# The low halves of the split weights made by ACT and an accumulating DMA, instead of a subtraction on DVE

## The chip, the core and the metric

The kernel runs on one core of a Trainium2 chip, as one program on one input (one sequence of 1024 frames, 1024 channels, one layer). The metric is the device time of one execution in microseconds (us). Of the kernel before there are three timed executions: 2161.12, 2165.23 and 2161.25 us, median 2161.25 us. One further execution was taken with the hardware profiler.

Five engines work side by side, each going through its own list of instructions in order: PE multiplies matrices, DVE does elementwise work, ACT does elementwise functions and copies, POOL does some elementwise work and here mostly starts DMA transfers, SP only starts transfers. An instruction that has to wait holds up everything behind it in its engine's list. A DMA that an engine starts runs on its own afterwards, on 16 DMA engines that all queues share.

## What is computed

The reference is one layer of a sequence model: a modulated RMS norm, one wide projection, a short convolution branch and a state-space (SSD) branch with a gated norm, two output projections merged by sigmoid gates, one more projection, and then a squared-ReLU MLP. Cut to what matters for the time:

```python
u = rms_norm(x, ln1) * (1.0 + scale1) + shift1          # scale, shift, gate: c_act @ w_ada + b_ada
proj = u @ w_in                                         # 1024 x 11296
gl, cb, cc, cx, z, xbc, dt = jnp.split(proj, split_at, axis=-1)
p_conv = (cb * causal_depthwise_conv(cc * cx, conv_w)) @ w_conv_out
y = ssd_scan(...) ; y = gated_norm(y * silu(z))
p_ssm = y @ w_ssm_out                                   # 2048 x 1024
g_conv, g_ssm = jnp.split(sigmoid(gl), 2, axis=-1)
x = x + gate1 * ((g_conv * p_conv + g_ssm * p_ssm) @ w_o)
u2 = rms_norm(x, ln2) * (1.0 + scale2) + shift2
x = x + gate2 * (square(relu(u2 @ w_up)) @ w_down)      # 1024 x 4096 and 4096 x 1024
return rms_norm(x, final_norm)
```

All of it is in float32. Nearly all of the time goes into the matrix products with weights.

## The kernel before, in words

**Layout.** Channels lie on the 128 partitions, frames along the free dimension: a tile of 128 channels by 1024 frames, mostly handled as two halves of 512. Weights come from memory in tiles of 128 x 1024 floats (512 KB): eight blocks of 128 x 128.

**Split operands.** PE multiplies in the float32r format, which rounds its inputs. To keep the accuracy, each operand is split in two: the high part is the operand rounded to float32r, the low part is the operand minus its high part, rounded in turn. A product is then the sum of three matmuls: high by high, high by low, low by high. Activations are split where they are made; the weights must be split in the kernel, tile by tile.

**How a weight is split.** `load_w` (lines 90 to 97) takes the next weight: SP starts the load of `wraw` (three buffers), ACT casts it to `whi` (line 94), and DVE computes `wlo` = `wraw` - `whi` (line 96, recorded under the helper's line 43). `whi` and `wlo` have four buffers each, so a new weight can be split as soon as PE has done its last matmul with an older one whose buffer it takes. In `proj` (matmuls at lines 111, 112 and 114), the weight's low part is needed after four matmuls with its high part: two for each of the two halves of the frames. One weight tile feeds 48 matmuls there.

**Strassen pairs.** The gate (`gl`), the `z`, four of the eight convolution tiles and most of the up projection run in pairs of weight tiles through `strassen_pair` (line 136), with Strassen's scheme of seven products instead of eight, 12 matmuls each (line 145), 84 a pair. There are 33 pairs: 5 for the gates, 8 for z, 6 for the convolution, 14 for the up projection. Each pair splits four weights in `wsplit` (lines 148 to 153): `wa` (a weight as loaded), `w12` and `w34` (two tiles of sums that DVE forms from the loaded ones in `s12` and `s34`), and `wb` (half a tile). The seven products follow in this order: P1 with `wa`, P2 and P3 with `w12`, P4 with `w34`, P5 with `wa`, P6 with `w34`, P7 with `wb`. The results are combined by DVE (`cu`, `cq`, `cy`) and written out by ACT.

**The conditioning product.** `gemvs` (line 412) multiplies 32 tiles of `w_ada` with a vector. POOL starts the load into `wv` (one buffer), DVE multiplies and sums (line 291, called here the gemv). They are issued three to a pair from the third gate pair on to the last z pair. The next load waits until DVE has done the gemv before it.

**Order of the work.** The source is written stage by stage, but the order within each engine's list is set when the program is built, by a scheduler that simulates the engines with its own idea of durations and puts an instruction where it became ready there. A change of one operation so moves others.

The stages in time: statistics and the first norm with the first four gate tiles (to about 80 us); gate tiles 4 and 5 (to 106); gate, z and convolution pairs (to about 485); per head group the projections and the SSD scan, with the other convolution tiles between (to about 1100); the two output projections and `w_o` (to about 1440); four up tiles and the 14 up pairs (to about 1800); the down projection and the last norm.

Of the kernel before, what the change touches and what calls it, by code (L numbers as in the profile page):

```python
# [7 lines left out]
F32 = mybir.dt.float32  # L8
# [3 lines left out]
ALU = mybir.AluOpType  # L12
# [4 lines left out]
T = 1024  # L17
H = 512
# [19 lines left out]
def hybrid_trunk(tc, xT, par, hrows, crow, wada1, wada2, win, wdt, wco, wso, wo, wup, wdn, out):  # L38
    nc = tc.nc
    pe, act, dve, pool, sp = nc.tensor, nc.scalar, nc.vector, nc.gpsimd, nc.sync  # L40

    def tt(o, a, b, op, eng=dve):
        return eng.tensor_tensor(out=o, in0=a, in1=b, op=op)  # L43

    def stt(o, a, s, b, op0, op1):
        return dve.scalar_tensor_tensor(out=o, in0=a, scalar=s, in1=b, op0=op0, op1=op1)  # L46
# [38 lines left out]
    def load_raw(src):  # L85
        raw = wp.tile([P, T], F32, name="wraw", bufs=3)
        sp.dma_start(raw, src)
        return raw

    def load_w(src, raw=None, eng=dve):  # L90
        if raw is None:
            raw = load_raw(src)
        hi = wp.tile([P, T], F32R, name="whi")
        act.copy(hi, raw)  # L94
        lo = wp.tile([P, T], F32R, name="wlo")
        tt(lo, raw, hi.bitcast(F32), ALU.subtract, eng=eng)
        return hi, lo

    def split(hi, lo, src):
# [3 lines left out]
    def shift_split(hi, lo, src, col):  # L103
        act.activation(hi, src, AF.Identity, bias=col)  # L104
        return stt(lo, src, col, hi.bitcast(F32), ALU.add, ALU.subtract)
# [3 lines left out]
    def mm3(outs, wh, wl, xh, xl, start, stop):  # L109
        for o, h_, l_ in zip(outs, xh, xl):  # L110
            pe.matmul(o, lhsT=wh, rhs=h_, start=start, stop=False)  # L111
            pe.matmul(o, lhsT=wh, rhs=l_, start=False, stop=False)  # L112
        for o, h_ in zip(outs, xh):
            last_mm[0] = pe.matmul(o, lhsT=wl, rhs=h_, start=False, stop=stop)  # L114
# [21 lines left out]
    def strassen_pair(tp_, w0, w1, X, evac):  # L136
        a, b, c, d = [mm.tile([P, H], F32, name="mm") for _ in range(4)]
        r0, r1 = load_raw(w0), load_raw(w1)
        k1, k2 = hs

        def prod(o, w, i, x, first, last):
            for k in range(4):
                s_ = slice(i * H + k * P, i * H + k * P + P)
                for j, (l_, r_) in enumerate(((w[0], x[k][0]), (w[0], x[k][1]), (w[1], x[k][0]))):
                    last_mm[0] = pe.matmul(o, lhsT=l_[:, s_], rhs=r_, start=first and k == j == 0,  # L145
                                           stop=k == 3 and j == 2, skip_group_check=True)

        def wsplit(src, n=T):
            hi = wp.tile([P, T], F32R, name="whi")[:, :n]
            act.copy(hi, src)  # L150
            lo = wp.tile([P, T], F32R, name="wlo")[:, :n]
            tt(lo, src, hi.bitcast(F32), ALU.subtract)
            return hi, lo

        wa = wsplit(r0)
        s12 = tp_.tile([P, T], F32, name="s12", bufs=1)
        s34 = tp_.tile([P, T], F32, name="s34", bufs=1)
        tt(s12[:, k1], r1[:, k1], r1[:, k2], ALU.add)
        tt(s12[:, k2], s12[:, k1], r0[:, k1], ALU.subtract)
        w12 = wsplit(s12)  # L160
        tt(s34[:, k1], r0[:, k1], r1[:, k1], ALU.subtract)
        tt(s34[:, k2], r0[:, k2], s12[:, k2], ALU.subtract)
        w34 = wsplit(s34)
        wb = wsplit(r1[:, k2], H)

        cu, cq, cy = [tp_.tile([P, H], F32, name=n) for n in ("cu", "cq", "cy")]
        prod(a, wa, 0, X["11"], True, False)
        act.copy(cu, a)  # L168
        prod(b, w12, 1, X["T2"], True, True)
        tt(cu, b, cu, ALU.add)  # L170
        prod(c, w12, 0, X["T1"], True, False)
        tt(cq, c, cu, ALU.add)
        prod(d, w34, 0, X["T3"], True, False)
        tt(cq, d, cq, ALU.add)
        evac(1, 1, cq)
        prod(a, wa, 1, X["21"], False, True)
        evac(0, 0, a)
        prod(c, w34, 1, X["22"], False, True)
        tt(cy, c, cu, ALU.add)
        evac(0, 1, cy)  # L180
        prod(d, wb, 0, X["T4"], False, True)
        tt(cu, d, cu, ALU.add)
        evac(1, 0, cu)
# [86 lines left out]
    wa = {}  # L270

    def load_ada(j):
        for q in (1, 0):
            wa[j, q] = p0.tile([P, T], F32, name="wada", bufs=8)
            sp.dma_start(wa[j, q], wada1[j, :, q])
# [6 lines left out]
    raws = [load_raw(win[f]) for f in (0, 1)]  # L282
# [7 lines left out]
    def gemv(w_, o):  # L290
        return dve.tensor_tensor_reduce(out=w_, in0=w_, in1=cb, scale=0.5, scalar=prm[:, BADA + o:BADA + o + 1],  # L291
                                        op0=ALU.mult, op1=ALU.add, accum_out=mcol[:, o:o + 1])
# [32 lines left out]
    ws = []  # L325
# [5 lines left out]
    for j in range(KT):  # L331
        if j > 1:
            load_ada(j)
        if j in (0, 1):
            with tc.issue_after(rdy.ins), (tc.issue_after(rbc.ins) if j else contextlib.nullcontext()):
                for f in range(2):
                    ws.append(load_w(win[2 * j + f], raws[2 * j + f]))
        with tc.issue_after(rdy.ins) if j else contextlib.nullcontext():
            gemv(wa[j, 1], 8 + j)
            gemv(wa[j, 0], j)  # L340
        stt(s1c[:, j:j + 1], mcol[:, 8 + j:9 + j], 1.0, prm[:, LN1 + j:LN1 + j + 1], ALU.add, ALU.mult)
        for h in (0, 1):
            x_ = xt[j][h]
            stt(x_, x_, s1c[:, j:j + 1], rbs[h], ALU.mult, ALU.mult)
            rdy = shift_split(uh[j][h], ul[j][h], x_, mcol[:, j:j + 1])
        if j == 0:
            continue
        for jj in ((0, 1) if j == 1 else (j,)):
            for h in (0, 1):
                for f in range(4):  # L350
                    mm3([sps[f][h]], ws[f][0][:, jj * P:jj * P + P], ws[f][1][:, jj * P:jj * P + P],
                        [uh[jj][h]], [ul[jj][h]], jj == 0, jj == KT - 1)
# [10 lines left out]
    p0.release()  # L363
    p0x.release()
    ws = [load_w(win[f]) for f in (4, 5)]
    tks, X = [], {n: [] for n in ("11", "21", "22", "T1", "T2", "T3", "T4")}
    dc1 = dcs[:, 8:12]
# [78 lines left out]
    for f in range(6, 16, 2):  # L446
        ts_ = [glp.tile([P, T], F32, name="glt") for _ in (0, 1)]

        def gl_ev(i, h, src):
            act.activation(ts_[i][:, hs[h]], src, AF.Tanh, scale=0.5)  # L450

        if f == 8:
            dt_chain()
        elif f > 8:
            gemvs(3)
        strassen_pair(pe1, win[f], win[f + 1], X, gl_ev)
        for i in (0, 1):
            act.dma_start(gl_d[f + i], ts_[i])
    for g in range(NG):
        ts_ = [glp.tile([P, T], F32, name="glt") for _ in (0, 1)]  # L460

        def z_ev(i, h, src):
            t = ts_[i][:, hs[h]]
            act.activation(t, src, AF.Tanh, scale=0.5)
            stt(t, t, 1.0, src, ALU.add, ALU.mult)

        gemvs(3)
        strassen_pair(pe1, win[gtile(g) + 4], win[gtile(g) + 5], X, z_ev)
        for i in (0, 1):
            act.dma_start(z_d[2 * g + i], ts_[i])  # L470
# [9 lines left out]
    for f0 in range(0, NYE, 2):  # L480
        ys_ = []
        for f in (f0, f0 + 1):
            y = glp.tile([P, T], F32, name="glt")
            v = pe1.tile([P, T + 32], F32, name="wv", bufs=1)
            pool.memset(v[:, 0:2], 0.0)
            keep = {}

            def v_ev(i, h, src):
                if (i, h) == (1, 1):
                    keep[0] = src  # L490
                elif (i, h) == (0, 0):
                    act.copy(y[:, hs[0]], src)
                else:
                    tt(v[:, 2 + H * h:2 + H * h + H], src, keep[0] if h else y[:, hs[0]], ALU.mult)

            strassen_pair(pe1, win[17 + 3 * f], win[16 + 3 * f], X, v_ev)
            taps(y, v, f)
            ys_.append(y)

        def y_ev(i, h, src):  # L500
            tt(ys_[i][:, hs[h]], src, ys_[i][:, hs[h]], ALU.mult)

        strassen_pair(pe1, win[18 + 3 * f0], win[21 + 3 * f0], X, y_ev)
        for i in (0, 1):
            act.dma_start(yc_d[f0 + i], ys_[i])
# [312 lines left out]
    ws = [load_w(wup[i]) for i in range(4)]  # L818
# [48 lines left out]
    for b in range(8):  # L867
# [21 lines left out]
        else:  # L889
            ws = [load_w(wdn[b, i]) for i in range(4)]  # L890
# [90 lines left out]
```

## Time and profile before

| | us |
|---|---|
| three timed executions | 2161.12, 2161.25, 2165.23 |
| the profiled execution's own time | 2164.64 |
| its span, first to last instruction | 2162.9 |
| PE busy | 2121.5 (98% of the span) |
| DVE busy | 1398.5 (65%) |
| ACT busy | 869.2 (40%) |
| POOL busy | 108.9 (5%) |

The span leaves 1.7 us of the profiled execution's time outside it. Busy times of PE overlap: a matmul of 128 x 512 is shown with about 390 ns, and the next one starts some 227 ns after it (between 345.83 and 346.51 us three matmuls start). So for PE a count of matmuls in a window tells more than its busy time: at full pace it does 222 or 223 in 50 us. The DMA share is the mean busy share of the 16 DMA engines.

### The profile page before, as it was taken

What the parts mean: (1) busy time and instruction counts of PE and PEld (TensorE: products, weight loads), DVE (VectorE), ACT (ScalarE), POOL (GpSimd) and SP (SyncE); (2) the same over time, 40 slices, a digit from 0 to 9 for tenths busy, and PEclk for the clock granted to TensorE, in tenths of its full rate; (3) what the DMA queues carried; (4) which work ended last, traced back from release to release, by engine and by line L of the source; (5) the groups of instructions that cost most, each with busy time, mean ns of one, the idle gap of its engine ahead of it and who ended that gap; (6) DMA issues with size and microseconds to landing.
All of it is one profiled execution on the core that took longest, in us unless ns stands there. A gap on an engine that the chain in (4) does not pass through costs nothing.

```text
span 2162.9 us, 26045 instructions
## 1 busy us (share of the span) xinstructions
PE 2121.5 (98%) x9920; PEld 1731.0 (80%) x9920; DVE 1398.5 (65%) x2144; ACT 869.2 (40%) x1436; POOL 108.9 (5%) x200
## 2 busy tenths in 40 slices
PE   7999999999999999999999999999999999999998
PEld 4778778888888888887878888888788888888887
DVE  7876787764786856767884658656655545444444
ACT  4433233334564636445663421334444453211212
POOL 0000000000000000000000000011000000000003
PEclk8999999999999999999999999999999999999999
DMA  8235654123233323233356676532333336422212
GB/s 303 74 106 194 201 180 165 60 87 110 63 98 108 83 93 103 71 109 91 98 184 230 224 265 212 196 126 90 131 111 117 108 117 224 124 90 88 88 39 78
DMA packets 115471, 283.27 MB, mean 131 GB/s; under 512 B 10465, under 2 KB 45665, under 8 KB 115346
## 3 DMA queue, kind: packets, MB, share of 16 engines
q1 hardware_dynamic: 86882, 187.02, 27.1%
q0 software_dynamic: 16192, 58.73, 8.0%
q10 hardware_dynamic: 12272, 35.85, 4.2%
q8 instruction: 78, 1.28, 0.2%
q14 instruction: 47, 0.39, 0.1%
HBM read 218.45 MB, written 63.11 MB: 130 GB/s over the span
## 4 chain that ended last, share of the span: by engine, by line
PE 81%; issue 11%; DVE 3%; DMA 2%; ACT 1%; POOL 1%; SPq 0%; POOLq 0%; DVEq 0%; ACTq 0%
PE mm L145 21%; PE mm L112 18%; PE mm L111 18%; PE mm L114 18%; PE B L600 2%; PE B L605 1%; PE C L622 1%; DMA wv<-in_wada 1%; DVE wada L291 1%; PE A L577 1%; DMA x<-in_xT 1%; POOL wv L415 1%; DVE ul L46 1%; DVE x L46 0%; DMA hr<-hid_d 0%
## 5 line engine op out<-in xcount | busy, mean ns | idle before, releaser
L111 PE MATMUL mm<-uh,whi 128*128 128x512 f32 x768 | 303.3, 398 | 3.7 <-ACT uh L104 3.2
L112 PE MATMUL mm<-ul,whi 128*128 128x512 f32 x768 | 304.7, 397 | 0.0
L94 ACT CAST whi<-wraw 128x1024 fp32r<-128x1024 f32 x125 | 131.4, 1051 | 428.4 <-PE mm L112 404.2
L145 PE MATMUL mm<-t,whi 128*128 128x512 f32 x944 | 292.2, 391 | 7.2 <-ACT whi L150 4.4
L114 PE MATMUL mm<-uh,wlo 128*128 128x512 f32 x768 | 246.2, 396 | 1.9 <-DVE wlo L43 1.9
L43 DVE TENSOR_TENSOR wlo<-wraw,whi 128x1024 fp32r<-128x1024 f32 (+1 forms) x191 | 215.6, 1129 | 40.6 <-ACT whi L94 34.3
L145 PEld LDWEIGHTS mm<-t,whi 128*128 128x128 f32 x944 | 177.4, 189 | 46.9 <-DVE cq L43 5.1
L46 DVE SCALAR_TENSOR_TENSOR y<-mm,mcol,y 128x512 f32<-128x512 f32 (+1 forms) x136 | 92.4, 715 | 158.0 <-PE mm L114 157.9
L145 PE MATMUL mm<-t,wlo 128*128 128x512 f32 x472 | 183.5, 390 | 0.0
L111 PEld LDWEIGHTS mm<-uh,whi 128*128 128x128 f32 x768 | 144.4, 189 | 35.7 <-ACT uh L104 5.3
L114 PEld LDWEIGHTS mm<-uh,wlo 128*128 128x128 f32 x768 | 144.8, 189 | 32.3 <-DVE wlo L43 2.3
L112 PEld LDWEIGHTS mm<-ul,whi 128*128 128x128 f32 x768 | 145.0, 189 | 29.4 <-issue 0.9
L112 PE MATMUL mm<-hid,whi 128*128 128x512 f32 (+1 forms) x416 | 154.9, 374 | 0.0
L111 PE MATMUL mm<-hid,whi 128*128 128x512 f32 (+1 forms) x416 | 153.9, 373 | 0.0
L111 PE MATMUL mm<-ys,whi 128*128 128x512 f32 x384 | 148.8, 397 | 2.3 <-DVE gt L46 1.8
L112 PE MATMUL mm<-ys,whi 128*128 128x512 f32 x384 | 149.0, 396 | 0.0
L46 DVE SCALAR_TENSOR_TENSOR cacc<-raw,hw,cacc 128x1024 f32<-128x1024 f32 x96 | 122.8, 1279 | 27.8 <-ACT cacc L552 27.4
L145 PE MATMUL mm<-s,whi 128*128 128x512 f32 x448 | 137.9, 389 | 0.7 <-ACT cu L168 0.7
L114 PE MATMUL mm<-hid,wlo 128*128 128x512 f32 (+1 forms) x416 | 130.0, 373 | 0.0
L114 PE MATMUL mm<-ys,wlo 128*128 128x512 f32 x384 | 122.6, 394 | 0.0
L594 ACT ACTIVATE seg<-acb,acum 128x128 f32<-128x128 f32 x256 | 81.9, 392 | 98.7 <-PE B L600 91.2
L43 DVE TENSOR_TENSOR wlo<-s,whi 128x1024 fp32r<-128x1024 f32 x66 | 80.5, 1220 | 52.4 <-ACT whi L150 52.4
(272 smaller groups left out, 3963.1 us busy)
## 6 DMA issues: line engine op xcount, KB each, us to landing
wraw<-in_win SPq DMA_DIRECT2D x87, 512.0 KB, 3.6
wv<-in_wada POOLq DMA_DIRECT2D x32, 512.0 KB, 3.8
acb<-ac_d SPq DMA_DIRECT2D x64, 256.0 KB, 4.6
wraw<-in_wup SPq DMA_DIRECT2D x32, 512.0 KB, 3.5
hr<-hid_d POOLq DMA_DIRECT2D x32, 512.0 KB, 4.6
wraw<-in_wdn SPq DMA_DIRECT2D x32, 512.0 KB, 3.5
hid_d<-hid POOLq DMA_DIRECT2D x28, 512.0 KB, 4.3
gt<-gl_d SPq DMA_DIRECT2D x24, 512.0 KB, 4.3
```

Source lines behind the costliest of these rows:

```text
L43: return eng.tensor_tensor(out=o, in0=a, in1=b, op=op)
L46: return dve.scalar_tensor_tensor(out=o, in0=a, scalar=s, in1=b, op0=op0, op1=op1)
L94: act.copy(hi, raw)
L111: pe.matmul(o, lhsT=wh, rhs=h_, start=start, stop=False)
L112: pe.matmul(o, lhsT=wh, rhs=l_, start=False, stop=False)
L114: last_mm[0] = pe.matmul(o, lhsT=wl, rhs=h_, start=False, stop=stop)
L145: last_mm[0] = pe.matmul(o, lhsT=l_[:, s_], rhs=r_, start=first and k == j == 0, stop=k == 3 and j == 2, skip_group_check=True)
L291: return dve.tensor_tensor_reduce(out=w_, in0=w_, in1=cb, scale=0.5, scalar=prm[:, BADA + o:BADA + o + 1], op0=ALU.mult, op1=ALU.add, accu ...
L415: pool.dma_start(w_, wada2[i])
L577: pe.matmul(A[:, 0:P], lhsT=bf[:, cs], rhs=cf[:, cs], start=True, stop=True)
L594: act.activation(seg[:, r, :], acb[:, r, :], AF.Relu, bias=acum[:, c, hd:hd + 1], scale=-1.0)
L600: pe.matmul(Bk[o:o + 64, P * (r // 2):P * (r // 2) + P], lhsT=xd[:, r, :], rhs=seg[:, r, :], start=True, stop=True, skip_group_check=True)
```

## The change

A new helper `low` takes the place of DVE's subtraction. ACT writes the negated value, rounded to float32r, into `wlo` (a multiply by -1, line 91 of the changed kernel); then POOL starts a DMA that reads the unsplit value once more and adds it to what is in `wlo` (line 92). The source of that DMA is the weight in memory for a weight as loaded, and the tile `s12` or `s34` in the core's own memory for the two sums of a pair. The four weights of the first stage keep the subtraction on DVE.

```diff
-    def load_w(src, raw=None, eng=dve):
+    def low(lo, val, src):
+        act.mul(lo, val, -1.0)
+        pool.dma_start(lo, src, accum_op=ALU.add)
+
+    def load_w(src, raw=None, eng=None):
         if raw is None:
             raw = load_raw(src)
         hi = wp.tile([P, T], F32R, name="whi")
         act.copy(hi, raw)
         lo = wp.tile([P, T], F32R, name="wlo")
-        tt(lo, raw, hi.bitcast(F32), ALU.subtract, eng=eng)
+        if eng is None:
+            low(lo, raw, src)
+        else:
+            tt(lo, raw, hi.bitcast(F32), ALU.subtract, eng=eng)
         return hi, lo
...
-        def wsplit(src, n=T):
+        def wsplit(val, src, n=T):
             hi = wp.tile([P, T], F32R, name="whi")[:, :n]
-            act.copy(hi, src)
+            act.copy(hi, val)
             lo = wp.tile([P, T], F32R, name="wlo")[:, :n]
-            tt(lo, src, hi.bitcast(F32), ALU.subtract)
+            low(lo, val, src)
             return hi, lo
 
-        wa = wsplit(r0)
+        wa = wsplit(r0, w0)
...
-        w12 = wsplit(s12)
+        w12 = wsplit(s12, s12)
...
-        w34 = wsplit(s34)
-        wb = wsplit(r1[:, k2], H)
+        w34 = wsplit(s34, s34)
+        wb = wsplit(r1[:, k2], w1[:, k2], H)
...
-                    ws.append(load_w(win[2 * j + f], raws[2 * j + f]))
+                    ws.append(load_w(win[2 * j + f], raws[2 * j + f], dve))
```

In the built program 254 splits change: 254 subtractions leave DVE (221 of a whole tile, 33 of half a tile), ACT gets 254 more instructions, POOL starts 254 more DMAs. 66 of them read from `s12` and `s34`, 188 from the weights in memory (33 of these half a tile).

Three places of the built order. The first is ACT's list over one z pair, before; the names `whi` and `wlo` carry the number of the tile, `glt` and `cq`, `cy`, `cu` are the results of the pair ahead, `mm` its sums on PE.

```order
L150 CAST whi_1955<-wraw_1951 128x1024
L464 ACTIVATE glt_1793<-cq_1834 128x512
L150 CAST whi_1963<-s12_1959 128x1024
L464 ACTIVATE glt_1792<-mm_1803 128x512
L150 CAST whi_1969<-s34_1960 128x1024
L464 ACTIVATE glt_1792<-cy_1835 128x512
L150 CAST whi_1973<-wraw_1953 128x512
```

And the same stretch in the changed program:

```order
L157 CAST whi_1985<-wraw_1981 128x1024
L91 ACTIVATE wlo_1987<-wraw_1981 128x1024
L471 ACTIVATE glt_1819<-cq_1864 128x512
L157 CAST whi_1994<-s12_1990 128x1024
L471 ACTIVATE glt_1818<-mm_1829 128x512
L91 ACTIVATE wlo_1996<-s12_1990 128x1024
L157 CAST whi_2001<-s34_1991 128x1024
L91 ACTIVATE wlo_2003<-s34_1991 128x1024
L471 ACTIVATE glt_1818<-cy_1865 128x512
L157 CAST whi_2006<-wraw_1983 128x512
L91 ACTIVATE wlo_2008<-wraw_1983 128x512
```

Each cast is followed by the negated rounding of the same value; for `w12` (the tile from `s12`) one write-out of the pair ahead stands between the two.

The second is POOL's list from the end of its setup on, before: all loads of `wv`, then small memsets.

```order
masks.py:66 AFFINE_SELECT tri<-tri 128x128
L415 DMA wv<-in_wada 128x1024 x32
L485 MEMSET wv 128x2 x4
L671 MEMSET vv 128x2 x2
L547 MEMSET raw 128x3 x11
```

And two z pairs of it in the changed program:

```order
L422 DMA wv_1968<-in_wada2 128x1024
L92 DMA wlo_1987<-in_win 128x1024
L422 DMA wv_1971<-in_wada2 128x1024
L92 DMA wlo_1996<-s12_1990 128x1024
L92 DMA wlo_2003<-s34_1991 128x1024
L422 DMA wv_1974<-in_wada2 128x1024
L92 DMA wlo_2008<-in_win 128x512
L422 DMA wv_2116<-in_wada2 128x1024
L92 DMA wlo_2135<-in_win 128x1024
L422 DMA wv_2119<-in_wada2 128x1024
L92 DMA wlo_2144<-s12_2138 128x1024
L92 DMA wlo_2151<-s34_2139 128x1024
```

The four accumulating DMAs of a pair and three loads of `wv` now share POOL's list, so a load that waits for its gemv stands ahead of a weight's low part, and the other way round.

The third is PE's list where the products with `w12` begin (P2 into the first sum, P3 into the second), before:

```order
L145 MATMUL mm_1947<-uh30_114,wlo_1957 128x512
L145 MATMUL mm_1948<-t10_678,whi_1963 128x512
L145 MATMUL mm_1948<-t11_679,whi_1963 128x512
L145 MATMUL mm_1948<-t10_678,wlo_1965 128x512
L145 MATMUL mm_1948<-t10_702,whi_1963 128x512
L145 MATMUL mm_1948<-t11_703,whi_1963 128x512
```

And in the changed program:

```order
L152 MATMUL mm_1977<-uh30_114,wlo_1987 128x512
L152 MATMUL mm_1978<-t10_680,whi_1994 128x512
L152 MATMUL mm_1978<-t11_681,whi_1994 128x512
L152 MATMUL mm_1979<-t00_676,whi_1994 128x512
L152 MATMUL mm_1979<-t01_677,whi_1994 128x512
L152 MATMUL mm_1978<-t10_680,wlo_1996 128x512
```

Two matmuls of P3 with the high part were drawn ahead of the first one with the low part of `w12`, which is now the fifth matmul with that weight instead of the third.

## The prediction

> **What bounds the kernel now.** The first view is the page's busy times, the second the list of what PE waited for (total us, times, longest).
>
> ```profile
> PE 2121.5 (98%) x9920; PEld 1731.0 (80%) x9920; DVE 1398.5 (65%) x2144; ACT 869.2 (40%) x1436; POOL 108.9 (5%) x200
> PE st L310 <- DVE sacc L43: 8.1, 2, 5.6
> PE mm L145 <- ACT whi L150: 4.4, 1, 4.4
> ...
> PE mm L145 <- DVE cq L43: 3.0, 5, 1.3
> ...
> PE mm L114 <- DVE wlo L43: 1.9, 1, 1.9
> PE mm L111 <- DVE gt L46: 1.8, 1, 1.8
> ...
> PE C L657 <- DVE sql L43: 1.4, 1, 1.4
> PE B L600 <- DVE seg L43: 1.0, 1, 1.0
> ```
>
> PE is the bound, 98% of the span. Its 15 waits add up to about 35 us, and those on DVE outside the opening statistics (`cq`, `wlo`, `gt`, `sql`, `seg`) to 9.1 us. That is all a lighter DVE can give back. So the question is not what DVE saves, but whether the new way delivers `wlo` in time, and what it loads the DMA engines with. The third view, busy time by windows, has PE's matmul count behind its busy time and the DMA share as the last but one column.
>
> ```profile
> 200.00:250.00 50.00, 48.36 (x212) 39.35 (x211) 35.33 (x53) 13.91 (x19) 4.24 (x8) 1.00 0.57 191
> 400.00:450.00 50.00, 50.00 (x223) 41.38 (x222) 34.46 (x46) 13.59 (x16) 0.10 (x1) 1.00 0.24 74
> 1370.00:1390.00 20.00, 20.00 (x90) 16.55 (x89) 15.81 (x24) 7.05 (x10) 0.00 (x0) 1.00 0.52 163
> 1650.00:1700.00 50.00, 50.00 (x222) 41.40 (x221) 27.20 (x35) 25.57 (x36) 2.66 (x5) 1.00 0.28 95
> 1700.00:1750.00 50.00, 50.00 (x222) 41.41 (x221) 25.64 (x34) 22.01 (x32) 2.66 (x5) 1.00 0.35 119
> ```
>
> 50 us hold 222 matmuls, so one takes 0.225 us, a product of 12 takes 2.7 and a Strassen pair of 84 takes 18.9 us. The first row is pairs with three gemvs: the DMA engines are already busy 0.57 x 18.9 = 10.8 us of each pair. The second is convolution pairs (4.5 us), the last two up pairs (0.315 x 18.9 = 6.0 us).
>
> **The change part by part.** What leaves DVE and what comes to ACT, at the durations of the same shapes:
>
> ```profile
> L43 DVE TENSOR_TENSOR wlo<-wraw,whi 128x1024 fp32r<-128x1024 f32 x158 | 193.1, 1222 | 40.6 <-ACT whi L94 34.3 <-ACT whi L150 4.2
> L94 ACT CAST whi<-wraw 128x1024 fp32r<-128x1024 f32 x125 | 131.4, 1051 | 428.4 <-PE mm L112 404.2 <-PE mm L145 18.2 <-issue 3.0
> L43 DVE TENSOR_TENSOR wlo<-wraw,whi 128x512 fp32r<-128x512 f32 x33 | 22.5, 682 | 0.0
> L150 ACT CAST whi<-wraw 128x512 fp32r<-128x512 f32 x33 | 20.4, 619 | 20.1 <-PE mm L145 18.7 <-ACT glt L450 1.4
> ```
>
> DVE: 221 x 1.222 + 33 x 0.682 = 293 us less. ACT: 221 x 1.051 + 33 x 0.619 = 253 us more, which takes it to 1122 us or 52%. Both lie beside PE's work; ACT's mostly falls into the 428 us it waits before `whi` for PE to free a buffer. I cost both at nothing in themselves; without that cover, one rounding on the path is 1.05 us per weight.
>
> The 254 DMAs have no row of their own kind. The nearest are these:
>
> ```profile
> q1 hardware_dynamic: 86882, 187.02, 27.1%
> q0 software_dynamic: 16192, 58.73, 8.0%
> wv<-in_wada POOLq DMA_DIRECT2D x32, 512.0 KB, 3.8
> pc<-at_d SPq DMA_DIRECT2D x8, 512.0 KB, 9.7
> L415 POOL DMA_DIRECT2D wv<-in_wada x32: 527/530/722, 152.7 to 342.7; - x32
> ```
>
> Queue q1 moves 187.02 MB in 27.1% of 2162.9 us, 586 us: 1.64 us for 512 KB on all 16 engines; q0 gives 1.54. I take 1.6 us of engine time. A plain POOL load of that size lands 3.8 us after its issue, and POOL's issuing takes 0.53 us (254 of them 135 us, on an engine that is idle 95%). Below, an accumulating DMA costs what a plain one does: 1.6 and 3.8 us. Above, I take the slowest landing of that size, 9.7 us, and count all of the excess over 3.8 as engine time: 7.5 us. Between them I take twice the plain engine time, 3.2 us, landing at 5.4 us, since such a transfer must read a second tile, the one it adds to; that is near the lower end.
>
> The Trainium skill has a rule that speaks against the change, on "Collectives: The Full Stack", section "The bandwidth ceiling: the fold count and why AG ≠ RS ≠ AR": a transfer that adds needs two source reads, and its rate is half that of a copy (32.35 against 62.28 GB/s there). By the nearest row, the plain load, the sum would be +4 us (first rival below), by the rule it is the forecast. No trace before shows which.
>
> In the pairs three costs count. First, latency. Buffers rotate so that `w12` is the tightest: it takes the buffer freed by P5 and is wanted by P2 of the next pair.
>
> ```profile
> 346.51 0.39 PE L145 MATMUL mm<-uh,whi 128*128 128x512 f32 x1
> 350.15 1.04 ACT L150 CAST whi<-s 128x1024 fp32r<-128x1024 f32 x1
> 351.09 0.59 ACT L464 ACTIVATE glt<-mm 128x512 f32<-128x512 f32 x1
> 351.58 1.04 ACT L150 CAST whi<-s 128x1024 fp32r<-128x1024 f32 x1
> 354.75 0.62 PE L145 MATMUL mm<-t,whi 128*128 128x512 f32 x2
> ```
>
> P6 begins at 346.51, P2 of the next pair at 354.75: 8.2 us, and its low part is wanted four matmuls later, at 9.1 us. The cast (0.94 to the next start), one write-out (0.49) and the rounding (1.04) use 2.5 us, which leaves 6.6 us for the DMA. At 3.8 or 5.4 us it is hidden; with a weight's load (1.6 us) on the engines at the same moment 5.4 becomes 7.0, a stall of 0.4. I put this at half of the 22 pairs without gemvs: +5 us. Other weights have more room: `wa` waits for P3 (10.8 us), projections outside the pairs work three weights of 10.8 us ahead.
>
> Second, engine time. A pair adds 3.5 transfers: at 3.2 us, 11.2 us. The 11 pairs with gemvs come to 10.8 + 11.2 = 22.0 us against 18.9, so they are paced by DMA: 11 x 3.1 = +34 us. Up pairs (17.2) and convolution pairs (15.7) still fit. In the `w_o` stage (third window row) a weight lasts 24 matmuls, 5.4 us, with 2.8 us of DMA; 3.2 more overruns by 0.6, over 16 weights 10 us, which the lead of three weights (16 us) covers.
>
> Third, three starts where the weights come fresh and nothing lies ahead:
>
> ```profile
> 79.55 1.06 ACT L94 CAST whi<-wraw 128x1024 fp32r<-128x1024 f32 x1
> 84.28 0.73 PE L114 MATMUL mm<-uh,wlo 128*128 128x512 f32 x2 [1.87 <-DVE wlo L43]
> 120.47 1.05 ACT L150 CAST whi<-s 128x1024 fp32r<-128x1024 f32 x1 [1.00 <-DVE s L43]
> 121.55 1.23 DVE L43 TENSOR_TENSOR wlo<-s,whi 128x1024 fp32r<-128x1024 f32 x1 [0.18 <-ACT whi L150]
> 1530.80 1.99 ACT L150 CAST whi<-s 128x1024 fp32r<-128x1024 f32 x2
> 1532.07 2.35 DVE L43 TENSOR_TENSOR wlo<-s,whi 128x1024 fp32r<-128x1024 f32 x2
> ```
>
> Gate tile 4: the rounding takes the place of the cast at 79.55, ends at 80.6, and the low part lands at 86.0 instead of being used at 84.28: +1.7 (plain +0.1). First gate pair: rounding to 122.5, landing 127.9 against 122.8: +5.1 (plain +3.5). First up pair: rounding to 1532.8, landing 1538.2 against 1533.3: +4.9 (plain +3.3). Together +11.7 (plain +6.9). The late thing after these is only the next product; the loss is not given back.
>
> Gain: the `cq` waits, where DVE sat in a gemv, -3 us. Sum: 34 + 5 + 12 - 3 = **+48 us**. The profiled execution took 2164.64 us, 1.7 us more than its span of 2162.9 and 3.4 us over the median of the timed runs; 2164.64 + 48 = 2212.6 for it, and 2161.25 + 48 = **2209 us** for the median.
>
> **The rivals.**
>
> Hidden all but the starts. If the accumulating DMA costs like a plain one, gemv pairs need 10.8 + 5.6 = 16.4 of 18.9 us and nothing is paced by DMA: 6.9 - 3 = +4, 2165 us. For it: 1.6 us is what both queues show. Against: it has to read twice.
>
> Faster. DVE's list is what PE waits for: 9.1 us by the list above. With DVE 293 us lighter they go, and where the scheduler draws other matmuls ahead at the starts (as the third order excerpt shows it doing once a pair) only some 3 us are lost: -6, 2155 us. It decides from a landing of 3.8 us or less on. Against: the start stalls alone eat most of it.
>
> DMA paces all pairs. At three times the plain engine time (4.8 us, 16.8 a pair): gemv pairs 27.6, 11 x 8.7 = 96; up pairs 22.8, 14 x 3.9 = 55; the other 8 pairs 21.3, 8 x 2.4 = 19; `w_o` 16 x 2.2 - 16 = 19; starts with a landing of 7.0 us 16.5; -3: +203, 2364 us. At the upper bound (7.5 us) gemv pairs become 37.1, up pairs 32.3, the rest 30.8: 200 + 188 + 95 and some 80 more, above 2700 us. For it: the 16 engines reach 0.95 at times even now, as the row below shows, so there is no reserve. Against: nothing shows so slow a transfer of 512 KB when alone.
>
> ```profile
> 1250.00:1270.00 20.00, 20.00 (x90) 16.57 (x89) 7.21 (x8) 4.55 (x7) 0.00 (x0) 1.00 0.95 338
> ```
>
> POOL's list. `wv` has one buffer, so load, gemv and next load run in a row; the 32 of them start from 152.7 to 342.7 us, 6.1 us apart, 18.4 a pair. With `wlo` transfers between and before them a landing that is 1.6 us longer makes 23.2 a pair: 11 x 4.3 = 47 in place of 34, 2222 us.
>
> That the change doesn't do what it says can be left aside: 254 subtractions are gone from the built list.
>
> **How the numbers follow.** About 0.2% (4.3 us) is what a measurement of this kernel can tell from no change. Forecast (1.5 to 2.5 times the plain engine time) 0.43; its own range from 2170 (1.5 times: 11 x 0.3 + 9 - 3) to 2252 (2.5 times: 11 x 5.9 + 14 x 1.1 + 14 - 3). Hidden 0.20, faster 0.08, DMA paces all 0.22, POOL's list 0.07. The range of 2160 to 2370 us holds the hidden case and goes to three times the engine time. Left out are the faster case and about half of "paces all". Faster: 0.08 and 0.02 of the hidden case, 0.10; same: 0.13 of the hidden case and 0.01 of the forecast, 0.14; slower: the rest, 0.76.
>
> **What would show it.** Right: the transfers of `wlo` land in 5 to 6 us where the engines are free; from the third gate pair to the last z pair the DMA share is 0.95 or more and PE counts about 190 matmuls in 50 us instead of 222; PE's list of waits is led by `wlo` from the DMA; up pairs run at 220 or more. Wrong on engine time: a landing near 3.8 us and a share of 0.87 there (hidden), or up pairs below 200 in 50 us and landings over 8 us (DMA paces all). Wrong on the list: DMA share below 0.9 in gemv pairs that are slow all the same, with POOL waiting for the gemv. The forecast falls if matmul counts in the gemv pairs stay at 222.

## The result and the profile after

The changed kernel takes **2230.74 us** (median; 2227.85 to 2234.24), the kernel before 2161.18 beside it: a ratio of 1.0321, 95% interval 1.0306 to 1.0336. Slower was forecast, at 2209 us. The profiled execution took 2234.24 us with a span of 2232.4, against 2162.9 before: 69.5 us more.

The page of the changed kernel, busy times and DMA queues:

```profile
PE 2141.1 (96%) x9920; PEld 1737.0 (78%) x9920; DVE 1133.8 (51%) x1890; ACT 1086.3 (49%) x1690; POOL 331.0 (15%) x454
q0 software_dynamic: 52768, 183.26, 38.5%
q1 hardware_dynamic: 86882, 187.02, 26.4%
```

PE does the same 9920 matmuls. It idles for 2232.4 - 2141.1 = 91.3 us instead of 41.4, and is busy 19.6 us longer: 50 us of the loss are idle time of PE, 20 are longer busy time (the last section says how much of that is the clock). DVE lost 265 us of work and ACT gained 217; neither shows in the time.

What PE waited for in the changed kernel (us in total, times, longest):

```profile
PE mm L152 <- DMA wlo<-s: 30.8, 11, 4.8
...
PE mm L152 <- DMA wlo<-in_win: 7.2, 7, 1.5
PE mm L121 <- DMA wlo<-in_win: 4.5, 1, 4.5
PE mm L118 <- DVE s L43: 4.3, 2, 2.7
...
PE mm L118 <- ACT ys L107: 3.7, 1, 3.7
...
PE mm L118 <- DVE y L46: 3.0, 2, 1.6
...
PE mm L152 <- DVE cq L43: 1.3, 3, 0.8
```

The list is led by `wlo` from the DMA: 42.5 us in 19 waits, none of which existed before. `cq` fell from 3.0 to 1.3.

Where the 69.5 us arise is seen from matmul counts. They were summed up window by window (25 us) in both kernels; for each moment of the kernel before, the lag is how much later the changed kernel reaches the same count:

| moment before, us | lag, us | what ran since the row above |
|---|---|---|
| 100 | 5.3 | opening, gate tiles 4 and 5 |
| 150 | 12.6 | first two gate pairs |
| 400 | 48.5 | the 11 pairs with gemvs, first convolution pair |
| 1100 | 48.6 | other convolution pairs, projections, SSD scan |
| 1400 | 60.0 | output projections, start of `w_o` |
| 1500 | 59.7 | rest of `w_o`, up tiles |
| 1600 | 65.2 | first up pairs |
| 1800 | 65.1 | the other up pairs |
| 1900 | 69.1 | start of the down projection |
| 2100 | 69.2 | down projection |

Half of the loss falls into the 250 us in which gemvs run; 700 us of projections and SSD and the steady up pairs lose nothing. Busy time by windows of the changed kernel (PE's matmul count in its brackets, the last three columns granted clock, DMA share and GB/s):

```profile
200.00:250.00 50.00, 43.10 (x177) 34.12 (x176) 20.66 (x33) 19.90 (x26) 10.41 (x14) 0.94 0.92 251
300.00:350.00 50.00, 43.60 (x187) 34.54 (x187) 24.85 (x40) 22.81 (x31) 10.62 (x15) 1.00 0.91 237
1650.00:1700.00 50.00, 50.00 (x222) 41.39 (x222) 16.86 (x26) 30.37 (x44) 12.82 (x17) 1.00 0.90 214
1700.00:1750.00 50.00, 50.00 (x222) 41.41 (x221) 15.46 (x23) 34.35 (x49) 13.12 (x18) 1.00 0.89 199
```

The first two rows are pairs with gemvs: 177 and 187 matmuls instead of 222 (203 in the 50 us between them). The last two are up pairs, at full pace with the **same DMA share**, 0.90. A share of 0.9 alone does not slow a pair, so the share of the slow pairs does not by itself explain them. This is what the experiments had to settle.

### The profile page after: what moved, and what is told of

It is laid out like the page before. It is cut to its first block, busy times and chain, and to the rows that moved or that the text cites. A ratio compares the mean times of both kernels' runs of the same rounds, so it can differ in the third digit from the quotient of the medians.

```text
span 2232.4 us, 26618 instructions
## 1 busy us (share of the span) xinstructions
PE 2141.1 (96%) x9920; PEld 1737.0 (78%) x9920; DVE 1133.8 (51%) x1890; ACT 1086.3 (49%) x1690; POOL 331.0 (15%) x454
## 3 DMA queue, kind: packets, MB, share of 16 engines
q0 software_dynamic: 52768, 183.26, 38.5%
q8 instruction: 78, 1.28, 0.2%
## 4 chain that ended last, share of the span: by engine, by line
PE 75%; issue 10%; DMA 9%; DVE 3%; POOL 2%; ACT 1%; SPq 0%; POOLq 0%; DVEq 0%; ACTq 0%
PE mm L152 19%; PE mm L118 16%; PE mm L121 16%; PE mm L119 16%; DMA yr<-y_d 2%; PE B L607 2%; DMA wlo<-s 1%; PE B L612 1%; POOL wlo L92 1%; PE C L629 1%; DMA hr<-hid_d 1%; DMA ccs<-yc_d 1%; PE A L584 1%; DVE yr L46 1%; POOL wv L422 1%
## 5 line engine op out<-in xcount | busy, mean ns | idle before, releaser
L98 ACT CAST whi<-wraw 128x1024 fp32r<-128x1024 f32 x125 | 131.3, 1050 | 350.9 <-PE mm L119 173.7
L152 PEld LDWEIGHTS mm<-t,whi 128*128 128x128 f32 x944 | 182.4, 194 | 43.5 <-ACT whi L157 5.1
L91 ACT ACTIVATE wlo<-wraw 128x1024 fp32r<-128x1024 f32 (+1 forms) x188 | 184.6, 982 | 0.0
L92 POOL DMA_DIRECT2D wlo<-in_win x84 | 73.7, 878 | 538.9 <-ACT wlo L91 433.3
L152 PEld LDWEIGHTS mm<-t,wlo 128*128 128x128 f32 x472 | 91.5, 194 | 54.9 <-DMA wlo<-s 35.8
```

The lines of the kernel that those rows point to most:

```text
L91: act.mul(lo, val, -1.0)
L92: pool.dma_start(lo, src, accum_op=ALU.add)
```

## The experiments

Where a diff shows `by_dma`, `low` chooses between ACT's rounding with the DMA (true) and the subtraction on DVE (false). "Lag" is taken as above.

### The pairs with gemvs alone

```diff
+    by_dma = [False]
+    def low(lo, val, src, hi):
+        if by_dma[0]: act.mul(lo, val, -1.0); pool.dma_start(lo, src, accum_op=ALU.add)
+        else: tt(lo, val, hi.bitcast(F32), ALU.subtract)
...
+        by_dma[0] = f > 8      # gate pairs from the third on, then all z pairs
...
+    by_dma[0] = False          # ahead of the convolution pairs
```

> The accumulating DMA only in the 11 pairs with gemvs; every other split subtracts on DVE as before. In the changed kernel the lag behind the kernel before grows by 36 us (12.6 to 48.5) while these pairs run. If the loss belongs to the pairs themselves (forecast: 11 x 3.1 = 34), this kernel takes 2161 + 34 to 36 = 2195 to 2197 us, with a matmul count near 185 in 50 us there and 222 everywhere else. If it is carried in from the starts ahead of them (a backlog of transfers that never clears), it stays below 2180.

Measured: 2199.81 us, ratio 1.0167 [1.0142, 1.0193]. The lag is 0.0 at 150 us, 36.2 at 400 and 34 from there to 2100. The loss belongs to these pairs; nothing is carried in from the starts.

### Only where the lag stayed flat

```diff
+    by_dma[0] = True           # convolution pairs; again from the head groups on
...
+    by_dma[0] = False          # ahead of the output projections
...
+        by_dma[0] = f > 4      # up pairs from the second on
...
+    by_dma[0] = False          # down projection
```

> The accumulating DMA only where the lag stayed flat: convolution pairs, the projections of the head groups, up pairs from the second on. The rest subtracts on DVE. If the loss sits in places, 2161 us (2158 to 2166). If a lighter DVE gives its waits back there (cq 3.0, sql 1.4, seg 1.0), 2156. If the loss is a general one of transfers that queue behind each other, which only showed in some places, 2170 or more.

Measured: 2162.92 us, ratio 0.9997 [0.9986, 1.0008]. In these places the change is free, and it gains nothing: the waits on DVE do not come back as time that can be measured. No version tried here beats the kernel before.

### wv loaded by SP

```diff
-            pool.dma_start(w_, wada2[i])
+            sp.dma_start(w_, wada2[i])
```

> The changed kernel, with the loads of wv started by SP instead of POOL: the same bytes on the same 16 engines, but no wlo transfer stands behind a wv load that waits for a gemv. Engine time (forecast, 22.0 us a pair whatever queue starts them): 2231 us, within 5. POOL's list (rival): pairs back at 18.9 us, 11 x 3.3 = 36 less, 2195. Both: the DMA share of 0.90 x 22.8 us leaves 20.5 us of engine time in a pair, so 11 x 2.3 = 25 less, 2206, with the share near 1.

Measured: 2235.34 us, ratio 1.0334 [1.0309, 1.0359]; lag 10.1 at 150 us, 47.4 at 400. The number is the forecast's. But PE waits for other things now. Its waits from 150 to 450 us in this kernel:

```profile
PE mm L152 <- DMA wlo<-s: 8.4, 6, 2.3
PE mm L152 <- DVE cy L43: 6.8, 2, 5.9
PE mm L152 <- DVE cq L43: 5.9, 5, 2.8
PE mm L152 <- DVE cu L43: 4.0, 2, 2.6
```

and DVE's, from 165 to 400 us:

```profile
DVE wv L298 <- DMA wv<-in_wada: 92.6, 27, 6.0
```

The wait moved from POOL's list to DVE's. There a gemv that waits for its `wv` stands ahead of `cu`, `cq` and `cy`, which PE wants. Taking `wlo` out from behind `wv` did not help, but the cycle of load, gemv and next load was still whole. So this run cannot tell engine time from that cycle.

### A plain transfer in place of the accumulating one

```diff
-        pool.dma_start(lo, src, accum_op=ALU.add)
+        pool.dma_start(lo, src)
```

> The changed kernel, with the accumulating DMA replaced by a plain one of the same bytes from the same source to the same tile on the same queue (the low part is then the whole weight, so the output is another). If the addition doubles the engine time (forecast), a 512 KB transfer falls from 2.9 to 1.6 us, a pair with gemvs needs 10.8 + 5.6 = 16.4 us and runs at full pace, landings are near 3.8 us and only the starts are left: about 2165 us. If the addition costs nothing and the loss is that of 124 MB more traffic, 2231. If POOL's list sets the pace, the pairs lose some 2 us each still: about 2190.

Measured: 2188.16 us, ratio 1.0108 [1.0077, 1.014]. Between the forecast's 2165 and the unchanged 2231: the addition itself costs 43 us, and some 24 stay, of which 15.6 in the pairs with gemvs. The total is near the 2190 that was set for POOL's list. The queues and the landings of this kernel, and after them the same rows of the changed kernel:

```profile
q0 software_dynamic: 52768, 183.26, 24.2%
...
wlo<-s POOLq DMA_DIRECT2D x66, 512.0 KB, 3.2
wlo<-in_win POOLq DMA_DIRECT2D x65, 512.0 KB, 4.7
wv<-in_wada POOLq DMA_DIRECT2D x32, 512.0 KB, 4.9
```

```profile
wlo<-s POOLq DMA_DIRECT2D x66, 512.0 KB, 6.0
wlo<-in_win POOLq DMA_DIRECT2D x65, 512.0 KB, 7.0
wv<-in_wada POOLq DMA_DIRECT2D x32, 512.0 KB, 5.6
```

This measures the disputed price. The 254 transfers are worth 237.5 of a whole tile. Queue q0 was busy 8.0% of 2162.9 = 173 us before, 24.2% of 2188.5 = 530 us here and 38.5% of 2232.4 = 859 us in the changed kernel: (530 - 173) / 237.5 = **1.50 us** for a plain transfer of 512 KB and (859 - 173) / 237.5 = **2.89 us** for an accumulating one, 1.93 times as much.

### Plain transfers and wv on SP

Both edits above at once.

> Both edits at once: plain transfers in place of the accumulating ones (the low part is then the whole weight, another output) and the wv loads started by SP. With plain transfers and wv on POOL the pairs with gemvs still lose 15.6 us (lag 4.4 to 20.0) at a DMA share of 0.77 to 0.81, where the engines are not the limit. If that remainder is POOL's list (a wlo transfer standing behind a wv load that waits for its gemv), it goes: 2188 - 15.6 = 2172 us. If it is the mere presence of the transfers or DVE's list behind the gemv, it stays: 2188. If POOL's list were all of the loss, the accumulating kernel with wv on SP would have shown it already; it did not (lag 10.1 to 47.4).

Measured: 2183.67 us, ratio 1.0096 [1.0074, 1.0117]. In the pairs with gemvs the lag grows by only 4.4 us (6.0 to 10.4) instead of 15.6. The total fell by 4.5 us, less than expected, since the starts came out worse here (6.0 against 4.4 at 150 us) and the output stages too. The 11 us between the two kernels go with the pace of the gemvs. In each of the next fences stands one row on the gemvs of one kernel (how many, durations in ns, first and last start). The kernel before:

```profile
L291 DVE CUSTOM_DVE_ANT_0 wv<-wv,cb,prm x21: 1274/1283/1287, 203.0 to 328.5; 128x1024 f32<-128x1024 f32 x21
```

The changed kernel:

```profile
L298 DVE CUSTOM_DVE_ANT_0 wv<-wv,cb,prm x12: 1283/1285/1286, 241.1 to 327.2; 128x1024 f32<-128x1024 f32 x12
```

Accumulating transfers, `wv` on SP:

```profile
L298 DVE CUSTOM_DVE_ANT_0 wv<-wv,cb,prm x13: 1277/1285/1286, 241.7 to 327.0; 128x1024 f32<-128x1024 f32 x13
```

Plain transfers, `wv` on POOL:

```profile
L298 DVE CUSTOM_DVE_ANT_0 wv<-wv,cb,prm x14: 1283/1285/1286, 242.8 to 329.6; 128x1024 f32<-128x1024 f32 x14
```

Plain transfers, `wv` on SP:

```profile
L298 DVE CUSTOM_DVE_ANT_0 wv<-wv,cb,prm x20: 1277/1284/1286, 204.2 to 325.0; 128x1024 f32<-128x1024 f32 x20
```

| kernel | us from gemv to gemv | three of them | loss of a pair (lag / 11) | median landing of `wv` | three cycles |
|---|---|---|---|---|---|
| before | 125.5 / 20 = 6.3 | 18.8 | 0 (18.9 long) | 3.8 | 16.1 |
| plain, SP | 120.8 / 19 = 6.4 | 19.1 | 0.4 | 4.4 | 17.3 |
| plain, POOL | 86.8 / 13 = 6.7 | 20.0 | 1.4 | 4.9 | 19.4 |
| changed, SP | 85.3 / 12 = 7.1 | 21.3 | 3.4 | 5.2 | 19.7 |
| changed | 86.1 / 11 = 7.8 | 23.5 | 3.3 (22.2 long) | 5.6 | 21.5 |

Three gemvs stand in each pair, so three steps are about as long as a pair whatever sets its length: the third column does not tell cause from effect. The last one is worked out without the pace, from the landing of a load, the gemv (1.28 us) and the time until the next load starts (some 0.3 us on POOL, 0.1 on SP): (3.8 + 1.28 + 0.3) x 3 = 16.1 for the kernel before, which leaves it room under 18.9. The kernels whose sum is over 18.9 are those that lose a microsecond or more. The changed kernel with `wv` on SP loses more than its sum says; PE waits there for `cy`, `cq` and `cu` as well. This is evidence for the cycle and no proof, since full engines lengthen the landing too; the last experiment cuts the cycle itself.

### The starts and the down projection alone

```diff
+    by_dma[0] = True           # gate tiles 4 and 5
...
+        by_dma[0] = f < 10     # first two gate pairs
...
+    by_dma[0] = True           # first four up tiles
...
+        by_dma[0] = f == 4     # first up pair
...
+    by_dma[0] = True           # down projection
```

> The accumulating DMA only at gate tiles 4 and 5, in the first two gate pairs (no gemvs), in the first four up tiles, the first up pair and the whole down projection; DVE elsewhere. Forecast: the three starts, +11.7, 2161 + 12 = 2173. By the lag of the changed kernel: 12.6 to the first pair with gemvs, 5.5 at the up projection and 4.0 at the start of the down projection, together 22: 2183. If stalls at starts are given back later, 2165 or less.

Measured: 2185.02 us, ratio 1.0101 [1.0081, 1.0122]. The lag is 11.2 at 150 us, grows by 7.9 from 1500 to 1600 and by 3.1 at the down projection; most of it stays to the end. The starts cost some 1.6 times what was forecast, 11.2 + 7.9 = 19 us against 11.7.

### The output stages alone

```diff
+    by_dma[0] = True           # from w_conv_out on
...
+    by_dma[0] = False          # ahead of the up projection
```

> The accumulating DMA only in the output projections (w_conv_out, w_ssm_out) and w_o, 40 weights; DVE elsewhere. Forecast: nothing, the lead of three weights covers 10 us of overrun, 2161. By the lag of the changed kernel (48.6 at 1100 us of the kernel before, 60.0 at 1400): 11.4, 2172. If that lag there came from transfers held up by the earlier stages, it is gone alone: 2161 to 2164.

Measured: 2183.94 us, ratio 1.0097 [1.008, 1.0115], more than the 11.4 us of the lag. Of the 17.9 us of lag here 12.4 arise between 1100 and 1150 us. This kernel's waits of PE there, and of DVE:

```profile
PE C L634 <- DVE xe L43: 8.8, 1, 8.8
```

```profile
DVE yr L46 <- DMA yr<-y_d: 11.9, 2, 8.4
```

`xe` stands on DVE behind `yr`, which waits for a load in a moment at which the DMA engines are full. The built order around it is another than in the changed kernel, so the sizes of single waits do not carry over. That the stage loses by itself does.

### ACT's roundings without the transfers

```diff
-        pool.dma_start(lo, src, accum_op=ALU.add)
+        tt(lo, val, lo.bitcast(F32), ALU.add)
```

> The changed kernel, with the DMA replaced by an addition on DVE of the same value to the same tile: ACT keeps its 254 negated roundings (253 us), DVE gets its 293 us back, no transfer is added. If ACT's instructions are hidden (forecast: they fall into the time it waits for PE's buffers), 2161 us (2158 to 2167): at the starts, one more instruction of 1.05 us stands before the low part, three times, +3. If ACT is late for its write-outs and holds PE, 2175 or more.

Measured: 2164.56 us, ratio 1.0007 [0.9995, 1.002]. ACT's 254 instructions are hidden. All of the loss is the transfers'.

### Up pairs with two transfers more, and the control

```diff
             pool.dma_start(hid_d[f + i], hid[i])
+            pool.dma_start(xtra[f - 4 + i], hid[i])
```

> The changed kernel, with each of the 28 hid tiles of the up pairs stored a second time, to a scratch tile that nobody reads: two plain transfers of 512 KB more in each of the 14 pairs, no wait added, no gemv and no wv load in these pairs. As changed, up pairs run at full pace with a DMA share of 0.89 to 0.90, 0.90 x 18.9 = 17.0 us of engine time a pair. If engine time is the limit (forecast), 17.0 + 2 x 1.6 = 20.2 us against 18.9: 14 x 1.3 = 18 more, 2231 + 18 = 2249, with fewer than 215 matmuls in 50 us there. If what counts in pairs is only when a transfer lands behind its own queue, the pairs stay at 222 and the time at 2231 to 2234.

> Control: the kernel before with the same second store of every hid tile. Its up pairs keep the DMA engines busy for 0.28 to 0.35 of 18.9 us, 6.0 us; 9.2 with the second stores. Engine time: no loss, 2161 to 2165. If the second store costs by holding the three hid buffers longer, it costs here too: 2170 or more, and the other run is to be read less that.

Measured: 2232.52 us, ratio 1.0332 [1.0306, 1.0359], and for the control 2162.78, ratio 1.0001 [0.9992, 1.0011]. No loss: a clear miss of the forecast's sum. The up pairs of this kernel, and then of the changed one:

```profile
1650.00:1800.00 150.00, 150.00 (x662) 123.80 (x661) 47.70 (x72) 96.95 (x136) 44.97 (x64) 1.00 1.00 262
```

```profile
1650.00:1800.00 150.00, 150.00 (x663) 124.20 (x663) 47.70 (x71) 94.65 (x135) 36.05 (x47) 1.00 0.89 209
```

The two stores raised the share by 0.11, that is 2.1 us of 18.9, not 3.2, and 209 GB/s to 262, while PE kept its pace. In the kernel before and in the control, at the same times, they raised it by 0.16, that is 3.0 us, close to the sum:

```profile
1650.00:1800.00 150.00, 150.00 (x664) 124.20 (x663) 77.95 (x97) 75.18 (x105) 9.36 (x18) 1.00 0.34 114
```

```profile
1650.00:1800.00 150.00, 150.00 (x664) 124.20 (x663) 76.04 (x95) 74.15 (x104) 18.00 (x34) 1.00 0.50 170
```

So busy times of single transfers add up while the engines have room, and no longer near a share of 1 (0.89 + 0.16 would be 1.05). A share of 0.9 is not yet full, 262 GB/s fit beside full-pace pairs, and the pairs with gemvs moved only 237 to 251.

### Gemvs spread over more pairs

```diff
-            gemvs(3)
+            gemvs(2)           # in all 11 pairs
...
+            gemvs(1)           # in each of four convolution pairs
...
+        gemvs(3)               # in each of the other two
```

> The changed kernel with its 32 gemvs spread wider: two instead of three in each of the 11 pairs, the other ten in the convolution pairs behind them (one in each of four, three in each of two). Engine time with a threshold at 18.9 us: 20.5 - 1.6 = 18.9 us a pair, so of the 36 us lost there 5 to 10 stay (POOL's list, which cost 11 with plain transfers, is two thirds as long), and the two pairs with three come to 15.3 + 4.9 = 20.2, +3: 2231 - 36 + 8 + 3 = 2206. If every gemv costs its share wherever it stands (36 / 32 = 1.1 us each, a wait on POOL's list and not a threshold), nothing is gained: 2231.

Measured: 2232.01 us, ratio 1.0316 [1.029, 1.0342]. The edit did not do what it says: the scheduler placed the loads as early as its own durations allowed, three a pair as before, so they only ended sooner. The lag grew from 13.0 to 36.2 by 350 us and then, in the convolution pairs with the rest, to 44.3 by 550. Some 31 us for 32 gemvs is what the expectation set against the forecast had said, a microsecond for each wherever it stands. But such a price is not shown: in the convolution pairs one wait of 3.9 us for `wlo` is most of what PE waits. Two gemvs a pair, held so by the order, was not tried.

### The cycle cut: wv in halves

```diff
+            if i == 0:
+                w_ = pe1.tile([P, T + 32], F32, name="wv", bufs=1)
+                thirds.extend([w_[:, hs[0]], w_[:, hs[1]], pe1.tile([P, H], F32, name="wx", bufs=1)])
+            for q in (0, 1):
+                w_ = thirds[(2 * i + q) % 3]
+                pool.dma_start(w_, wada2[i][:, hs[q]])
...
```

The gemv follows on each half, the second adding to the first; each is ordered behind the last sum of the pair ahead, which keeps three gemvs to a pair.

> The changed kernel, with each load of wv and each gemv cut into two halves of 512 columns that go round three half buffers: still three gemvs a pair, the same bytes, the same queue (POOL's). Only the loop is cut in which a load waits for the gemv before it: in the changed kernel a gemv starts every 7.8 us in these pairs (12 from 241.1 to 327.2 us), three make 23.4, against 6.3 us before; with three half buffers two loads are under way while one is used. If this loop paces the pairs (the rival called POOL's list), 2231 - 36 + some 5 = 2200 us. If engine time does (forecast), the bytes are the same: 2231.

Measured: 2210.08 us, ratio 1.0225 [1.0207, 1.0243]: 21 us less than the changed kernel, with the same bytes on the same queue. The lag in these pairs grows by 12.0 us (8.5 to 20.5) instead of 36. From 160 to 390 us, this kernel and then the changed one:

```profile
160.00:390.00 230.00, 219.88 (x938) 173.53 (x937) 127.97 (x261) 108.95 (x147) 72.69 (x107) 1.00 0.99 262
```

```profile
160.00:390.00 230.00, 200.72 (x838) 159.24 (x837) 110.81 (x175) 98.37 (x130) 51.94 (x70) 0.97 0.91 240
```

and what PE waits for, in this kernel, from 165 to 400 us:

```profile
PE mm L153 <- DMA wlo<-s: 9.3, 18, 0.9
```

With the cycle cut the share rises from 0.91 to 0.99 and a pair takes 18.9 + 12.0 / 11 = 20.0 us. So the gemvs' cycle, at 22.2 us a pair, lay over something else at 20.0. The edit also changes where the gemvs stand in DVE's list; what that alone is worth was not run.

What is left is probably engine time: a pair needs 0.91 x 22.2 = 20.2 us of it in the changed kernel and 0.99 x 20.0 = 19.8 here, more than 18.9. This is argued and not shown. Up pairs ran at full pace with a share of 1.00 and the same 262 GB/s, and DVE now waits longest for transfers that still read the one buffer of `s12` or `s34`, a second cycle that no run cut:

```profile
DVE s L43 <- DMA wlo<-s: 37.4, 15, 4.8
```

## Why the prediction was right in its size and wrong in a cause

**The price of the transfer: right.** Twice the plain engine time was chosen, 3.2 us; 2.89 was measured, 1.93 times the 1.50 of a plain one in the same place. The rule that the prediction took from the Trainium skill ("Collectives: The Full Stack", section "The bandwidth ceiling: the fold count and why AG ≠ RS ≠ AR": there a collective that adds has half the rate of one that copies) agrees with this measurement. The landing was chosen too short: 5.4 us, and 6.0 (from `s12` and `s34`) and 7.0 (from memory) were measured.

**The second cost of the pairs (+34): size right, mechanism wrong.** 36 us were lost there. The step said that the sum of engine times, 22.0 us, paces the pair. That step failed: the engines were at 0.88 to 0.92, not at 0.95 or more, and with the same bytes a pair took 20.0 us once the cycle was cut. That 34 is so near to 36 is luck. The sign named for the rival, a share below 0.9 with POOL waiting for the gemv, came close. POOL's largest wait from 165 to 400 us:

```profile
POOL wv L422 <- DVE mcol L298: 147.0, 26, 9.8
```

By itself that sign says little: the kernel before waits so too, 159.9 us in 29 times from 150 to 350 us, and loses nothing. What paced the pairs, as the cut shows, is the mechanism given as the rival "POOL's list": one `wv` buffer, so load, gemv and next load run in a row. The load's landing grew from 3.8 to 5.6 us, the step from gemv to gemv from 6.3 to 7.8. That rival had said 23.2 us a pair and 2222 us in all; it was given a chance of 0.07. Engine time is likely the second limit, 20.0 us a pair and 12 us in all; the sum for it, 22.0, was too high. The rival's name was too narrow as well: with `wv` on SP's queue the loss stayed, and the cycle was still whole there, through the lists of SP and DVE.

**The first cost, latency (+5): did not come.** Convolution and up pairs without gemvs lose nothing; in the up pairs the change leaves 222 matmuls in 50 us. The 6.6 us worked out for `w12` did cover a landing of 6.0.

**The third cost, the starts (+11.7): too small.** 12.6 us to the first pair with gemvs and 5.5 at the up projection, 18 in all. At gate tile 4 the rounding did not take the place of the cast but came after it and a write-out, and the transfer, beside others, landed at 88.9 instead of 86.0: a wait of 4.5 us. From 50 to 165 us PE waits 10.6 us, against 3.3 from 50 to 155 before; these 7.3 us are near the 6.8 that the first two starts had in the sum. Some 2 us more are the clock, below, a term that was left out; the last 3 are not traced.

**The `w_o` stage (0): right; the output projections ahead of it: left out.** The lag grows by 11.4 us between 1100 and 1400 us, but `w_o` begins only near 1385. The last matmul with the low part of a weight and `ys`, the input of the output projections, starts at 1384.5 in the kernel before and at 1444.3 in the changed one (first and last start stand behind the three durations); the lag of 60 does not grow in `w_o`.

```profile
L114 PE MATMUL mm<-ys,wlo x384: 387/389/628, 1097.7 to 1384.5; 128*128 128x512 f32 x192
```

```profile
L121 PE MATMUL mm<-ys,wlo x384: 387/389/632, 1144.2 to 1444.3; 128*128 128x512 f32 x192
```

So most of the prediction's window row from 1370 to 1390 lies ahead of `w_o`, and the output projections had no term. Their weights come in time: PE never waits for `wlo` between 1100 and 1400 us. It waits for `s` (4.3), `ys` (3.7 and 2.4) and `xe` (1.8). `s` and `ys` stand in the lists of DVE and ACT behind other loads: for `yr` alone DVE waits 21.0 us there, against 9.2 from 1050 to 1350 in the kernel before. The down projection's start loses 4 us (PE waits 3.0 for `y`); it was not in the sum either.

**The gain (-3) did not show:** `cq` gave 1.7, and the kernel with the change in the free places alone is within 0.1% of the kernel before.

**What was costed at nothing** held: ACT's 254 roundings are hidden, and DVE's relief is worth nothing that can be measured.

Together: 36 for 34, 0 for 5, 18 for 12, 11 and 4 for stages without a term, nothing for -3: 69 in place of 48. The direction and the largest term carried the forecast, the latter by luck; most of its 21 us of shortfall are starts and stages that were left out.

## What to carry to other kernels

Before adding transfers, look for each place where one buffer makes a load, its use and the next load run in a row, and compare so many of these cycles, landing included, with the time of the work they stand beside: here 3 x 5.4 = 16.1 us beside 18.9, so a landing could grow by 0.9 us for nothing, and the 1.8 us that it grew by could not all be hidden. A lead on the weights protects only the weights; ask of every other load of the stage what it waits for. And near a full share do not take a sum of single transfers' busy times for a bound: add a transfer and see whether the pace falls.

## What the runs showed of the hardware that was not expected

An accumulating transfer also costs its issuer more: POOL spends 0.88 us on it, and 0.53 on a plain transfer of the same tiles. The group of the 84 whose source is a whole tile or half of one of the projection's weights, on the page of the changed kernel, and then, as shortest, median and longest in ns, with plain transfers:

```profile
L92 POOL DMA_DIRECT2D wlo<-in_win x84 | 73.7, 878 | 538.9 <-ACT wlo L91 433.3
```

```profile
L92 POOL DMA_DIRECT2D wlo<-in_win x84: 527/530/720, 80.2 to 1056.0; - x84
```

A stall of PE can cost more than its length, because the granted clock falls with it. The changed kernel around the stall of 4.81 us that ends at 177.1:

```profile
174.00:176.00 2.00, 0.00 (x0) 0.00 (x0) 0.04 (x2) 0.00 (x0) 1.43 (x2) 1.00 1.03 233
176.00:178.00 2.00, 0.90 (x2) 0.81 (x3) 0.86 (x2) 0.00 (x0) 0.00 (x0) 0.50 1.05 279
178.00:180.00 2.00, 2.00 (x6) 1.52 (x6) 1.03 (x2) 1.14 (x2) 0.00 (x0) 0.50 1.05 283
180.00:182.00 2.00, 2.00 (x7) 1.52 (x6) 1.75 (x3) 0.08 (x1) 0.00 (x0) 0.50 1.08 281
182.00:184.00 2.00, 2.00 (x8) 1.58 (x7) 1.37 (x3) 0.00 (x0) 0.56 (x1) 0.79 0.65 254
```

After it 2 us hold 6 or 7 matmuls instead of 9, at a clock of 0.50, for some 6 us. About half of the 19.6 us of longer busy time come from this: 119 matmuls start in stretches at half the clock and keep PE busy for 51.3 us, against 65 and 28.7 before; at 0.225 us each that is 24.5 us too long against 14.1, 10 more. The rest is not traced. The Trainium skill ("TensorE: Matmul & The Clock Gate", section "HAM oscillation — how this bites in real kernels") warns of idle gaps above about 3.4 us; the stalls of 4.46 and 4.81 us agree. The length alone does not decide here, though: stalls of 2.02, 2.28 and 2.64 us in the pairs left the clock at 1.00, while in the kernel before stalls of 0.95 us (to 119.4), 1.81 (to 1128.7) and 1.87 (to 84.3) were followed by half a clock too. The last of them:

```profile
84.00:86.00 2.00, 1.72 (x6) 1.45 (x7) 2.00 (x4) 2.00 (x6) 0.00 (x0) 0.83 0.29 88
86.00:88.00 2.00, 2.00 (x6) 1.52 (x6) 2.00 (x5) 1.12 (x4) 0.00 (x0) 0.50 0.92 315
```

Why these were enough is open.
